# Chunk ends and first stage of a two-layer fp32 decoder rearranged: gate/up behind the down slabs, four plain pairs, squares on ScalarE

## Chip, cores and metric
One core of a Trainium2 chip runs the whole program. The metric is the device time in microseconds (us), here of single executions; the trace is one profiled execution of the kernel before.

## What is computed
Two macaron layers over 528 tokens (16 learned ones and 512 inputs) of width 1024, all in float32. FFN is a SwiGLU of inner width 2816, 22 slabs of 128.

```
def swiglu(x, w_gate, w_up, w_down):
    return (jax.nn.silu(x @ w_gate) * (x @ w_up)) @ w_down
...
h = concat(meta, x)
for l in range(2):
    h = h + 0.5 * swiglu(rmsnorm(h, ffn1_norm[l]), ...)
    h = h + mix(rmsnorm(h, mix_norm[l])) @ w_out[l]
    h = h + 0.5 * swiglu(rmsnorm(h, ffn2_norm[l]), ...)
y = rmsnorm(h, final_norm)[:, 16:]
```

(The loop is abridged; mix is a retention group beside a differential attention group. The change leaves it alone.)

## The kernel before
**Number format.** An fp32 product is made of three float32r matmuls: ScalarE copies the high half of an operand (`split`, L108, for weights; L327 for the inputs XH), VectorE subtracts for the low half (L109, and XL in L328), and TensorE adds hi x hi, lo x hi and hi x lo.

**Stages.** There are four FFN stages (two a layer), called stage 1 to 4 here, and a mix stage behind the first and the third. In each FFN stage, gate and up of one slab m of the inner width are a **pair**: two weight slabs of 512 KB, which `gu(m)` uses. The first PLAIN = 2 pairs of a stage are plain (`plain`, L518, 96 matmuls of 264 columns). All others go by one level of Strassen-Winograd: seven products P1 to P7 of four k steps and three matmuls each, 84 in all (`product`, L496), which `evacuate` adds up from PSUM: u1, u2 and u4 are copies on ScalarE (L455), L469 adds P2, L474 adds P5 into U, L476 and L477 make the gate from P3, L480 adds P4 and L481 multiplies; `split_hidden` makes the two halves hh (ScalarE, L551) and hl (VectorE, L552) of the result. Its weights need sums S1 to S4 of the quarters, which `sums` makes step by step: VectorE L129, L130 and L132, GpSimd L133.

**Chunks.** The 22 slabs are worked in three chunks, which end at 8, 16 and 22 (6, 14 and 22 in the last stage). After a chunk, `down` multiplies its hidden slabs by eight slabs of the down weights (L280), and evacuates each with L586 (times r/2) and L589 (added to h). `ffn_steps` sets the order: gate and up go one pair ahead, so that pair b of the next chunk runs before the down step of (a, b), and P5, P3 and P4 of that pair n come behind the down step, among the products of pair n + 1.

**Weights.** The class `Weights` goes down one list, `plan`, with three counters: transfers begun (`advance_dma`, four raw tiles of 512 KB, RAW_BUFS), splits made, slabs used. `step` is called between products and makes one step of the next slab's work; `take` hands a slab over. Tile pools set what waits for what, and a scheduler reorders the instructions of each engine within that.

**The start.** `start` loads the first slab in two halves between the inputs h[k]. Then, in a pool of their own, the inputs are scaled and split (`post_pair`), squared for the norm (`post_sq`: GpSimd squares six of eight slabs, L364, and adds with VectorE in turn, L369) and summed for Strassen (`post_sums`, L347 to L350), all before stage 1 begins. `norm_end` makes r = 1/rms (L413 last), which the first evacuation needs (L542).

```
for k in PAIRED:
    post_sq(k, FULL, k == 0, k == KD - 1, False, k % 4 < 3)
for k in range(4):
    post_sums(k, FULL, scratch)
```

## Time and profile before
| | |
|---|---|
| three runs | 2095.88, 2097.12, 2102.14 us; median 2097.12 |
| profiled execution | 2096.26 us, span 2094.5 us |
| mean granted TensorE clock | 0.992 of full speed |
| TensorE | 15238 matmuls, busy 2006.8 us |
| VectorE | 2292 instructions, busy 1573.0 us |
| ScalarE | 1506 instructions, busy 965.7 us |
| GpSimd | 286 instructions, busy 410.0 us |

The span runs from the first to the last instruction of the trace; the execution's own time is 1.8 us longer. A busy time is the sum of the engine's instructions; of TensorE, whose matmuls overlap and whose ends are modelled, the starts are the safer reading. Idle time counts only on the engine that the rest waits for.

### The profile page before, as it was taken

To read this page: it belongs to the slowest core of one execution; us is meant where nothing else is said; L and a number is where in the kernel's file an instruction comes from. 1 tells how busy PE (TensorE), PEld (TensorE's weight loads), DVE (VectorE), ACT (ScalarE), POOL (GpSimd) and SP (SyncE) were. 2 spreads that over 40 slices of the span, in tenths; PEclk is the share of its full clock that TensorE was granted. 3 is DMA by queue.
4 is the path that set the end of the run, shared out by engine and by line. 5 is a ranking of instruction groups with operands and counts; after the bars stand their busy time and mean duration, and the time that the engine had idled before them with its cause. 6 is when DMAs were issued, how large, how long until landed. Compare 5 with 4: busy or idle time off the path is not lost. (4 is left out here: it accounts for less than half of the span.)

```text
span 2094.5 us, 36936 instructions
## 1 busy us (share of the span) xinstructions
PE 2006.8 (96%) x15238; PEld 1930.9 (92%) x15238; DVE 1573.0 (75%) x2292; ACT 965.7 (46%) x1506; POOL 410.0 (20%) x286
## 2 busy tenths in 40 slices
PE   6999999999999999999989999999999999999996
PEld 5899999999999999999989999999888879898995
DVE  8867857668777886867698587766778789696765
ACT  5533525445446552543565254344554465353443
POOL 4100000344343100100110010004434331010002
PEclk8999999999999999999999999999999999999998
...
GB/s 153 91 131 52 121 81 95 120 68 64 57 61 90 89 123 70 95 129 68 94 102 102 91 91 116 67 99 114 66 62 62 70 81 101 101 101 121 80 104 49
DMA packets 57656, 190.08 MB, mean 91 GB/s; under 512 B 7056, under 2 KB 9104, under 8 KB 57488
## 3 DMA queue, kind: packets, MB, share of 16 engines
...
q8 instruction: 119, 1.95, 0.4%
q10 hardware_dynamic: 1024, 1.08, 0.3%
...
## 5 line engine op out<-in xcount | busy, mean ns | idle before, releaser
L133 POOL TENSOR_TENSOR ws<-ws,wraw 128x512 f32<-128x512 f32 x80 | 118.7, 1484 | 1101.0 <-DVE ws L132 931.8
L108 ACT ACTIVATE whi<-wraw 128x1024 fp32r<-128x1024 f32 (+1 forms) x180 | 184.8, 1032 | 274.7 <-PE pm L280 149.2
L496 PE MATMUL pm<-XH,xhi 128*128 128x264 f32 (+1 forms) x848 | 243.2, 287 | 11.0 <-DVE gu L474 5.4
L496 PE MATMUL pm<-XH,xlo 128*128 128x264 f32 (+1 forms) x848 | 240.5, 284 | 0.0
L496 PE MATMUL pm<-XL,xhi 128*128 128x264 f32 (+1 forms) x848 | 240.4, 283 | 0.0
L496 PE MATMUL pm<-XH,whi 128*128 128x264 f32 (+1 forms) x752 | 215.6, 287 | 6.8 <-DVE gu L474 6.6
L496 PE MATMUL pm<-XH,wlo 128*128 128x264 f32 (+1 forms) x752 | 213.1, 283 | 0.0
L496 PE MATMUL pm<-XL,whi 128*128 128x264 f32 (+1 forms) x752 | 213.0, 283 | 0.0
L109 DVE TENSOR_TENSOR wlo<-wraw,whi 128x1024 fp32r<-128x1024 f32 (+1 forms) x148 | 186.2, 1258 | 25.1 <-ACT whi L108 24.4
L280 PE MATMUL pm<-XH,whi 128*128 128x264 f32 (+1 forms) x768 | 181.1, 304 | 9.1 <-DVE ra L668 8.2
L280 PE MATMUL pm<-XL,whi 128*128 128x264 f32 (+1 forms) x768 | 178.7, 301 | 0.0
L280 PE MATMUL pm<-XH,wlo 128*128 128x264 f32 (+1 forms) x768 | 178.7, 302 | 0.0
L496 PEld LDWEIGHTS pm<-XH,xhi 128*128 128x128 f32 x848 | 159.5, 188 | 16.3 <-DVE gu L474 7.9
L496 PEld LDWEIGHTS pm<-XH,xlo 128*128 128x128 f32 x848 | 159.8, 188 | 0.3
L496 PEld LDWEIGHTS pm<-XL,xhi 128*128 128x128 f32 x848 | 159.9, 189 | 0.0
L496 PEld LDWEIGHTS pm<-XH,whi 128*128 128x128 f32 x752 | 141.4, 188 | 9.8 <-DVE gu L474 8.9
L496 PEld LDWEIGHTS pm<-XH,wlo 128*128 128x128 f32 x752 | 141.7, 188 | 0.2
L496 PEld LDWEIGHTS pm<-XL,whi 128*128 128x128 f32 x752 | 141.7, 188 | 0.0
L280 PEld LDWEIGHTS pm<-XH,whi 128*128 128x128 f32 x768 | 123.8, 189 | 16.9 <-issue 4.1
L108 ACT ACTIVATE xhi<-ws 128x1024 fp32r<-128x1024 f32 x84 | 88.9, 1058 | 103.7 <-PE pm L496 37.1
L108 ACT ACTIVATE whi<-ws 128x1024 fp32r<-128x1024 f32 x76 | 80.5, 1059 | 108.9 <-PE pm L496 45.2
L280 PEld LDWEIGHTS pm<-XL,whi 128*128 128x128 f32 x768 | 123.4, 189 | 4.7
...
## 6 DMA issues: line engine op xcount, KB each, us to landing
...
```

Of the source, the lines that this page charges most:

```text
L108: self.nc.scalar.activation(out=hi, in_=t, func=AF.Copy)
L109: (eng or self.nc.vector).tensor_tensor(out=lo, in0=t, in1=hi.bitcast(F32), op=ALU.subtract)
L133: nc.gpsimd.tensor_tensor(out=s4, in0=s2, in1=a12, op=ALU.add)
L280: nc.tensor.matmul(out=ps[:, o:o + c1 - c0], lhsT=a, rhs=b[:, c0:c1], start=start and n == 0, stop=stop and n == 2,)
L496: nc.tensor.matmul(out=out_, lhsT=p[:, s], rhs=q, start=k == 0 and n == 0 and what in ("P1", "P2", "P7"), stop=k == 3 and n == 2, skip_gro ...
```

## The change
- **Order of use.** `ffn_steps` now gives gate and up of a chunk, then its down step. The first pair of the next chunk runs behind the down slabs, but it is put into the list of transfers after DOWN_LEAD = 3 of the eight down slabs, and its sums are made during the down step. A second list, `use`, holds the order of use, and `step`, `ready` and `take` go by it.
- **Chunk ends.** P5, P3 and P4 of the chunk's last pair come among the first two slabs of the down step (`part`, `done`): half of slab 0 behind P5, the rest but the last k behind P3, slab 1 but its last k behind P4, then the last k of both.
- **Plain pairs.** Gate and up take turns at each of the eight input slabs (before: all of gate, then all of up). In stage 1 four pairs are plain (PLAIN_FIRST), two more than before: 24 matmuls more in all.
- **Start.** The first weight slab is one transfer ahead of the inputs, the second comes after two of them. Inputs are prepared in the pool of stage 1. The squares are on ScalarE, the adds all on VectorE, and `post_sums` comes behind the first plain pair.
- **Splits** of down slabs take their tiles from one pool in turn with the others (`parts_tile(False)`).

The diff, cut to its core:

```diff
@@ -41,15 +41,16 @@
 PLAIN = 2
+PLAIN_FIRST = 4
+DOWN_LEAD = 3
...
-    a = done = 0
+    a = 0
     for b in FFN_CHUNKS[kind]:
-        while done < min(b + 1, KF):
-            yield "gu", done
-            done += 1
+        for m in range(a, b):
+            yield "gu", m
         yield "down", (a, b), b == KF
@@ -64,8 +65,12 @@
-    def __init__(self, nc, pool, plan, ahead, dma_ahead):
-        self.nc, self.pool, self.plan = nc, pool, plan
+    def __init__(self, nc, pool, plan, use, ahead, dma_ahead):
+        self.nc, self.pool, self.plan, self.use = nc, pool, plan, use
+        self.turn_of = {i: u for u, i in enumerate(use)}
         self.ahead, self.dma_ahead = ahead, dma_ahead
@@ -74,16 +79,6 @@
-    def start(self):
-        srcs, n, kind = self.plan[0]
-        self.raw[0] = [self.raw_tile() for _ in srcs]
-        self.n_dma = 1
-        for t, src in zip(self.raw[0], srcs):
-            for c in (slice(0, 512), slice(512, 1024)):
-                self.nc.sync.dma_start(out=t[:, c], in_=src[:, c])
-                yield
@@ -161,7 +156,7 @@
                 )
-            parts = self.parts_tile(kind == "ffn")
+            parts = self.parts_tile(False)
             self.split([p[:, :n] for p in parts], t[:, :n], nc.gpsimd if kind == "mix" and i % 2 else None)
@@ -173,30 +168,34 @@
         i = self.n_split
-        if self.hold or i >= len(self.plan) or i > self.n_used + self.ahead:
+        if self.hold or i >= len(self.plan):
             return False
-        if self.plan[i][2] != "pair":
+        pair = self.plan[i][2] == "pair"
+        first = pair and self.plan[self.use[self.turn_of[i] - 1]][2] != "pair"
+        if self.turn_of[i] > self.n_used + (9 if first else 1 if pair else self.ahead):
+            return False
+        if not pair:
             self.advance_split(i + 1)
-        elif i <= self.n_used + (1 if self.plan[i - 1][2] == "pair" else 3):
+        else:
+            if first:
+                self.turn = 3
             self.n_split += 1
...
             next(self.gen)
-        else:
-            return False
         return True
     def ready(self, i):
-        while self.n_split <= i or self.gen is not None and self.at == i:
+        while i not in self.parts or self.gen is not None and self.at == i:
             assert self.step(), (i, self.n_split, self.n_used)
     def take(self):
-        i = self.n_used
-        if self.plan[i][2] == "pair":
-            self.ready(i)
-        else:
-            self.advance_split(i + 1 + self.ahead)
+        i = self.use[self.n_used]
+        upto = max(self.use[self.n_used:self.n_used + 1 + self.ahead]) + 1
+        if self.plan[i][2] != "pair":
+            self.advance_split(upto)
+        self.ready(i)
         self.n_used += 1
-        self.advance_dma(i + 1 + self.ahead + self.dma_ahead)
+        self.advance_dma(upto + self.dma_ahead)
         return self.parts.pop(i)
@@ -212,7 +211,10 @@
-    plan = []
+    def n_plain(l, f):
+        return PLAIN if l or f else PLAIN_FIRST
+    plan, use = [], []
     for l in range(DEPTH):
@@ -223,15 +225,20 @@
                     m, = args
-                    if m < PLAIN:
+                    if m < n_plain(l, f):
                         plan += [((wgu[l, f, m, i],), 1024, "plain") for i in range(2)]
+                    elif m not in FFN_CHUNKS[stage_kind(l, f)]:
+                        plan.append(((wgu[l, f, m, 0], wgu[l, f, m, 1]), 1024, "pair"))
                     else:
-                        plan.append(((wgu[l, f, m, 0], wgu[l, f, m, 1]), 1024, "pair"))
+                        at = len(plan) - KD + DOWN_LEAD
+                        plan.insert(at, ((wgu[l, f, m, 0], wgu[l, f, m, 1]), 1024, "pair"))
+                        use += [*range(len(use), at), *range(at + 1, len(plan)), at]
                 else:
...
                         plan.append(((wd[l, f, m, :, a * 128:b * 128],), (b - a) * 128, "ffn"))
-    W = Weights(nc, const, plan, 2, 2)
+    use += range(len(use), len(plan))
+    W = Weights(nc, const, plan, use, 2, 2)
@@ -353,19 +360,17 @@
-    def post_sq(m, mode, first, end, last=False, pool_squares=False):
+    def post_sq(m, mode, first, end, last=False, on_vector=False):
...
             nc.vector.tensor_tensor(out=sq, in0=hm, in1=hm, op=ALU.mult)
-        elif pool_squares:
-            nc.gpsimd.tensor_tensor(out=sq, in0=hm, in1=hm, op=ALU.mult)
         else:
...
         if not first and not apart:
-            add = nc.vector if end or pool_squares and m % 2 else nc.gpsimd
+            add = nc.vector if end or on_vector else nc.gpsimd
             add.tensor_tensor(out=total, in0=total, in1=sq, op=ALU.add)
@@ -431,7 +436,7 @@
-    def ffn(l, f, mode, g_next, kind):
+    def ffn(l, f, mode, g_next, kind, first=None):
         with tc.tile_pool(name=f"ffn{l}{f}", bufs=1, reuse_waits="tile") as pool:
@@ -449,6 +454,9 @@
+            if first is not None:
+                first(scratch)
@@ -503,6 +511,8 @@
+            np = n_plain(l, f)
@@ -521,14 +531,17 @@
-                if m < PLAIN - 1:
-                    for x in range(2):
-                        for i in range(0, KD, 2):
-                            half(x, 0, PAIRED[i:i + 2])
-                            half(x, 1, PAIRED[i:i + 2])
-                        if m == 0 and x == 0:
-                            norm_end(mode)
-                            act_table(SILU)
+                if m < np - 1:
+                    for k in PAIRED:
+                        for x in range(2):
+                            half(x, 0, (k,))
+                            half(x, 1, (k,))
+                    if m == 0:
+                        norm_end(mode)
+                        act_table(SILU)
+                        if first is not None:
+                            for k in range(4):
+                                post_sums(k, mode, scratch)
                 else:
@@ -560,39 +573,62 @@
             def gu(m):
-                if m < PLAIN:
+                if m < np:
                     plain(m)
-                    if m == PLAIN - 1:
+                    if m == np - 1:
                         for k in range(4):
                             post_t4(k, mode)
-                elif m == PLAIN:
-                    begin(m)
+                    return
+                begin(m)
+                n = m - 1
+                if n in state:
+                    rounds((("P5", n), ("P1", m), ("P2", m), ("P3", n), ("P6", m), ("P4", n), ("P7", m)))
+                else:
                     rounds((("P1", m), ("P2", m), ("P6", m), ("P7", m)))
-                else:
-                    begin(m)
-                    n = m - 1
-                    rounds((("P5", n), ("P1", m), ("P2", m), ("P3", n), ("P6", m), ("P4", n), ("P7", m)))
...
                 c0, c1 = ab
-                if final:
-                    n = KF - 1
-                    rounds((("P5", n), ("P3", n), ("P4", n)))
-                    act_table(LNEXP)
-                srcs = [hidden.pop(m) for m in range(c0, c1)]
+                n, nk = c1 - 1, c1 - c0
+                order = down_order(kind, final)
+                srcs = [hidden.pop(m) for m in range(c0, n)]
+                banks = {}
                 W.hold = final
-                for i, (m, md) in enumerate(down_order(kind, final)):
-                    P = project(md, srcs, ("pm", "pa")[i % 2])
+                def part(j, k0, k1):
+                    md = order[j][1]
+                    if j not in banks:
+                        banks[j] = pair(("pm", "pa")[j % 2]), W.take()
+                    ps, chunk = banks[j]
+                    for k in range(k0, k1):
+                        accumulate(ps, md, srcs[k:k + 1], chunk, k, nk)
+                        if k % 2:
+                            W.step()
+                def done(j):
+                    m, md = order[j]
+                    P = view(banks.pop(j)[0], md)
                     nc.vector.scalar_tensor_tensor(
...
                     nc.vector.tensor_tensor(out=cols(h[m], md), in0=cols(h[m], md), in1=P, op=ALU.add)
-                    if not final:
-                        W.step()
-                        continue
-                    post_h(m, g_next, md, kind, scratch)
-                    if g_next == 3 * DEPTH and m == KD - 1:
-                        finish(md)
+                    if final:
+                        post_h(m, g_next, md, kind, scratch)
+                        if g_next == 3 * DEPTH and m == KD - 1:
+                            finish(md)
+                product("P5", n)
+                part(0, 0, nk // 2)
+                product("P3", n)
+                part(0, nk // 2, nk - 1)
+                product("P4", n)
+                if final:
+                    act_table(LNEXP)
+                srcs.append(hidden.pop(n))
+                part(1, 0, nk - 1)
+                for j in range(len(order)):
+                    part(j, nk - 1 if j < 2 else 0, nk)
+                    done(j)
@@ -1005,12 +1041,12 @@
-    first = W.start()
-    next(first)
     nc.sync.dma_start(out=gain, in_=gains)
-    for k in PAIRED:
+    W.advance_dma(1)
+    for i, k in enumerate(PAIRED):
         nc.sync.dma_start(out=h[k], in_=hT[k])
-        next(first, None)
+        if i == 1:
+            W.advance_dma(2)
     W.advance_dma(4)
@@ -1021,18 +1057,17 @@
     act_table(LNEXP)
-    with tc.tile_pool(name="first", bufs=1, reuse_waits="tile") as pool:
-        scratch = lambda m: free_scratch(pool, m)
+    def first_inputs(scratch):
         W.advance_split(2)
...
         for k in PAIRED:
-            post_sq(k, FULL, k == 0, k == KD - 1, False, k % 4 < 3)
-        for k in range(4):
-            post_sums(k, FULL, scratch)
+            post_sq(k, FULL, k == 0, k == KD - 1, on_vector=True)
...
         last = l == DEPTH - 1
-        ffn(l, 0, FULL, 3 * l + 1, "mix")
+        ffn(l, 0, FULL, 3 * l + 1, "mix", None if l else first_inputs)
         if l == 0:
```

How the instructions move, at the three places that the prediction speaks of (of the kernel before and of the changed one, whose line numbers differ: L335 is the old L328, L354 to L357 the old L347 to L350, L374 the old L369, L104 the old L109, L504 the old L496, L565 the old L552, L611 and L614 the old L586 and L589).

First, VectorE's first instructions, before:

```order
L347 TENSOR_TENSOR xt<-xb_107 128x264
L109 TENSOR_TENSOR wlo<-wraw,whi 128x1024
L328 TENSOR_TENSOR XL<-xb_107,XH 128x528
L348 TENSOR_TENSOR xt<-xb_111,xb_107 128x264
L349 SCALAR_TENSOR_TENSOR xt<-xt,xb_111 128x264
L347 TENSOR_TENSOR xt<-xb_115 128x264
L348 TENSOR_TENSOR xt<-xb_119,xb_115 128x264
L350 SCALAR_TENSOR_TENSOR acc1h<-xt,xb_111 128x264
L328 TENSOR_TENSOR XL<-xb_111,XH 128x528
```

and now:

```order
L104 TENSOR_TENSOR wlo<-wraw,whi 128x1024
L354 TENSOR_TENSOR xt<-hh_106 128x264
L355 TENSOR_TENSOR xt<-ws_110,hh_106 128x264
L356 SCALAR_TENSOR_TENSOR xt<-xt,ws_110 128x264
L374 TENSOR_TENSOR acc<-acc,sq 128x528
L357 SCALAR_TENSOR_TENSOR acc1h<-xt,ws_110 128x264
L335 TENSOR_TENSOR XL<-hh_106,XH 128x528
L335 TENSOR_TENSOR XL<-ws_110,XH 128x528
L104 TENSOR_TENSOR wlo<-wraw,whi 128x1024
```

The first lo half of weights stands ahead of the sums (xt), and the adds of squares (acc) are among the first instructions, each on VectorE, where GpSimd squared and added beside it.

Second, TensorE in stage 1's third chunk, at the end of P1 of one pair (before pm_3569, now pm_3542) and the beginning of P3 of the pair ahead of it. Before:

```order
L496 MATMUL pm_3569<-XH_62,xlo_3396 128x264
L496 MATMUL pm_3569<-XL_63,xhi_3395 128x264
L496 MATMUL pa_3706<-XH_62,whi_3494 128x264
L496 MATMUL pa_3706<-XH_62,wlo_3495 128x264
L496 MATMUL pa_3706<-XL_63,whi_3494 128x264
L496 MATMUL pa_3706<-XH_62,whi_3494 128x264
L496 MATMUL pa_3706<-XH_62,wlo_3495 128x264
L496 MATMUL pa_3706<-XL_63,whi_3494 128x264
L496 MATMUL pm_3433<-XH_62,xhi_3389 128x264
```

and now:

```order
L504 MATMUL pm_3542<-XH_62,whi_3335 128x264
L504 MATMUL pm_3542<-XH_62,wlo_3336 128x264
L504 MATMUL pm_3542<-XL_63,whi_3335 128x264
L504 MATMUL pm_3410<-XH_62,xhi_3329 128x264
L504 MATMUL pm_3410<-XH_62,xlo_3330 128x264
```

Six matmuls of the next pair's P2 (pa) stood between the two, behind five others of it ahead of P1; now P3 follows P1 directly, and P2 stands elsewhere.

Third, VectorE at the final down step of stage 1. Slab 0's and 1's evacuations are those of the first pm and pa. Before:

```order
L552 TENSOR_TENSOR hl5_3970<-gu_3850,hh5_3969 128x528
L586 SCALAR_TENSOR_TENSOR pm_3974<-pm_3974,r_71 128x528
L586 SCALAR_TENSOR_TENSOR pa_4018<-pa_4018,r_71 128x528
L589 TENSOR_TENSOR slabs_61<-slabs_61,pm_3974 128x528
L109 TENSOR_TENSOR wlo_4170<-wraw_4073,whi_4169 128x768
L586 SCALAR_TENSOR_TENSOR pm_4068<-pm_4068,r_71 128x528
L589 TENSOR_TENSOR slabs_61<-slabs_61,pa_4018 128x528
L109 TENSOR_TENSOR wlo_4220<-wraw_4123,whi_4219 128x768
```

and now:

```order
L565 TENSOR_TENSOR hl5_3972<-gu_3819,hh5_3971 128x528
L611 SCALAR_TENSOR_TENSOR pm_3909<-pm_3909,r_71 128x528
L611 SCALAR_TENSOR_TENSOR pa_3976<-pa_3976,r_71 128x528
L614 TENSOR_TENSOR slabs_61<-slabs_61,pm_3909 128x528
L104 TENSOR_TENSOR wlo_3978<-wraw_3786,whi_3977 128x768
L611 SCALAR_TENSOR_TENSOR pm_4037<-pm_4037,r_71 128x528
L614 TENSOR_TENSOR slabs_61<-slabs_61,pa_3976 128x528
L104 TENSOR_TENSOR wlo_4039<-wraw_3910,whi_4038 128x768
```

Slabs counted from 0, the lo half behind the first add was that of slab 6 (wlo_4170); now it is that of slab 3 (wlo_3978), whose first matmuls stand 12 matmuls behind the last of slab 0 on TensorE.

## Rows read from the trace of the kernel before

**Rows 1.** The page: busy us (share of the span) x instructions.

```profile
PE 2006.8 (96%) x15238; PEld 1930.9 (92%) x15238; DVE 1573.0 (75%) x2292; ACT 965.7 (46%) x1506; POOL 410.0 (20%) x286
```

**Rows 2.** Stretches: length, busy us by engine, granted clock, DMA share, GB/s.

```profile
core 0: us, PE busy (x) PEld busy (x) DVE busy (x) ACT busy (x) POOL busy (x), PEclk, DMA share, GB/s
7.72:54.58 46.86, 32.17 (x197) 30.06 (x197) 45.34 (x60) 26.23 (x38) 23.24 (x11) 0.85 0.41 146
20.50:36.30 15.80, 8.38 (x35) 7.72 (x35) 15.80 (x20) 3.55 (x5) 8.16 (x5) 0.57 0.21 66
54.58:120.84 66.26, 62.77 (x505) 61.72 (x505) 55.79 (x81) 35.49 (x55) 7.17 (x6) 1.00 0.29 93
120.84:174.90 54.06, 54.06 (x446) 54.06 (x445) 30.24 (x40) 13.14 (x16) 2.57 (x2) 1.00 0.29 92
174.90:254.80 79.90, 76.84 (x613) 75.18 (x612) 68.76 (x96) 42.67 (x64) 8.17 (x6) 1.00 0.29 96
307.00:353.00 46.00, 45.84 (x374) 45.41 (x373) 38.95 (x57) 24.79 (x38) 3.87 (x3) 1.00 0.26 85
712.00:777.00 65.00, 62.42 (x506) 61.58 (x505) 55.02 (x81) 34.27 (x53) 6.53 (x5) 1.00 0.30 94
```

**Rows 3.** TensorE, 0 to 55 us: start, length, instruction [idle before, releaser].

```profile
7.72 0.59 PE L518 MATMUL pm<-XH,whi 128*128 128x264 f32 x1 [7.72 <-ACT XH L327]
...
15.13 0.59 PE L518 MATMUL pm<-XL,whi 128*128 128x264 f32 x1 [4.16 <-DVE XL L328]
...
26.32 0.59 PE L518 MATMUL pm<-XL,whi 128*128 128x264 f32 x1 [5.77 <-DVE XL L328]
...
54.58 0.36 PE L496 MATMUL pm<-XH,xhi 128*128 128x264 f32 x1 [2.02 <-DVE gu L542]
```

**Rows 4.** VectorE, 5 to 33 us, the same columns.

```profile
11.02 1.53 DVE L349 SCALAR_TENSOR_TENSOR xt<-xt,xb 128x264 f32<-128x264 f32 x1
...
14.99 0.42 DVE L349 SCALAR_TENSOR_TENSOR xt<-xt,xb 128x264 f32<-128x264 f32 x1
...
15.96 0.70 DVE L369 TENSOR_TENSOR acc<-acc,sq 128x528 f32<-128x528 f32 x1
...
17.54 0.97 DVE L328 TENSOR_TENSOR XL<-xt,XH 128x792 fp32r<-128x792 f32 x1
...
27.65 1.82 DVE L328 TENSOR_TENSOR XL<-xb,XH 128x528 fp32r<-128x528 f32 x1
...
30.07 1.21 DVE L109 TENSOR_TENSOR wlo<-wraw,whi 128x1024 fp32r<-128x1024 f32 x1
31.21 0.69 DVE L328 TENSOR_TENSOR XL<-xb,XH 128x528 fp32r<-128x528 f32 x1
```

**Rows 5.** GpSimd, 16 to 23 us, the same columns.

```profile
16.73 5.52 POOL L364 TENSOR_TENSOR sq<-slabs 128x528 f32<-128x528 f32 x1 [3.26 <-DVE acc L369]
```

**Rows 6.** DMA in 0 to 30 us, 40 equal slices.

```profile
GB/s 0 0 131 265 203 266 301 309 296 372 335 403 408 424 422 432 410 426 377 379 246 22 0 0 0 0 0 0 0 0 0 0 0 0 93 333 273 0 0 0
```

**Rows 7.** TensorE at a stop in stage 1 and one in stage 2.

```profile
191.88 0.39 PE L496 MATMUL pm<-XH,xhi 128*128 128x264 f32 x1 [1.69 <-DVE gu L474]
...
735.41 0.39 PE L496 MATMUL pm<-XH,whi 128*128 128x264 f32 x1 [1.30 <-DVE gu L474]
```

**Rows 8.** TensorE's waits, 712 to 777 us: in total, times, longest.

```profile
PE pm L496 <- DVE gu L474: 2.6, 4, 1.3
```

**Rows 9.** VectorE at a wait in stage 1's second chunk.

```profile
189.57 0.69 DVE L130 TENSOR_TENSOR ws<-wraw 128x512 f32<-128x512 f32 x1 [3.41 <-DMA wraw<-in_wgu]
```

**Rows 10.** VectorE at the final down step of stage 1.

```profile
379.32 0.72 DVE L586 SCALAR_TENSOR_TENSOR pm<-pm,r 128x528 f32<-128x528 f32 x1 [2.90 <-PE pm L280]
379.95 0.71 DVE L586 SCALAR_TENSOR_TENSOR pa<-pa,r 128x528 f32<-128x528 f32 x1
380.56 0.69 DVE L589 TENSOR_TENSOR slabs<-slabs,pm 128x528 f32<-128x528 f32 x1
381.17 0.95 DVE L109 TENSOR_TENSOR wlo<-wraw,whi 128x768 fp32r<-128x768 f32 x1
```

## The prediction

> **What bounds the kernel now.** I read the page's busy line first: TensorE is busy 96% of the span [rows 1], so time is lost only where TensorE stands or runs at its lower clock. Next, the table by stage [rows 2], for where TensorE stands. The stretch 120.84 to 174.90 has no idle time at all: 446 matmuls in 54.06 us, a pace of 0.1212 us for 264 columns. I take that pace for full speed and call **excess** what a stretch lasts beyond matmuls times pace. It is 46.86 - 197 x 0.1212 = 23.0 us in stage 1's plain pairs, and by the same sum 5.0 us in the pairs behind them, 5.6 in its second chunk, 0.7 in its third, and 3.7 in the first chunk of stage 2. The down stretch itself has none.
>
> The start's rows say why. TensorE begins at 7.72 us, stops for 4.16 us before 15.13 and for 5.77 us before 26.32, both times for a lo half from VectorE (XL, L328), and once more for 2.02 us before the first Strassen product at 54.58, on the gate's evacuation L542 [rows 3]. In 20.5 to 36.3 VectorE is busy all the 15.80 us and the granted clock is 0.57, which is a mix of 1.2 GHz, the lower of two levels, and 2.4 GHz [rows 2]. VectorE is slow there because GpSimd squares beside it: one and the same sum (L349) takes 1.53 us at 11.02 and 0.42 at 14.99 [rows 4], while one square stretches to 5.52 us [rows 5].
>
> **The start.** First matmul: the other 256 KB of the first weight slab now land ahead of h[0]; at the 203 to 266 GB/s of these first microseconds [rows 6] that is 1.0 to 1.3 us, so the first matmul moves from 7.72 to about 9.
>
> VectorE's list, from the order: up to the eighth XL of the inputs it holds three 128x1024 lo halves, 14 sums of 264 columns, 8 XL of 528, two of 792, five adds of 528 and little else. Undisturbed rows give 1.21, 0.42, 0.69, 0.97 and 0.70 us [rows 4], less the 0.08 by which neighbours overlap (1.14 from 30.07 to 31.21): 3.4 + 4.8 + 5.0 + 1.8 + 3.1 = 18.1 us, from 6.5 to about 25, where the old kernel has its last such XL at 31.21. Taking the squares off GpSimd is what does it: nine VectorE instructions beside it, to the XL of 1.82 us at 27.65, lasted some 0.8 to 1.1 us longer than alone, as the two L349 show: about 8.6 in all. Against that, all seven adds now stand on VectorE, where three did: 4 x 0.62 = 2.5 us more. Squares go to ScalarE, busy 26.23 of 46.86 us [rows 2]; eight more fit beside VectorE's list and cost nothing, unless an add waits for its square.
>
> One section speaks against this. The Trainium skill, "Perfetto Trace Analysis", section "Optimizing Scalar/DVE Operations", says that a saturated VectorE may be relieved by giving work to ScalarE or even GpSimd, with the reservation that GpSimd shares VectorE's port. By its first half the change would only lose the 2.5 us; by its reservation, and the rows, it gains.
>
> TensorE then takes gate and up in turn per slab, so each XL feeds 12 matmuls instead of 6, and it no longer comes to an XL before it is made: by 28 us the first 100 matmuls are through, at full clock by about 22. Behind them 288 plain matmuls wait for nothing but r, whose chain now starts with the adds at once. I allow 1.0 us for that wait, and the 2.02 us wait at 54.58 goes, as two more plain pairs cover r's chain. 28 + 288 x 0.1212 + 1.0 = 64 us. The Strassen pairs 4 to 7 follow, 336 x 0.1212 = 40.7 us, with about 2 us of stalls: 107. The old kernel has 700 of its matmuls behind it at 120.84, and these are 724, so the 24 extra matmuls of two plain pairs (2.9 us) are inside. **Start: -14 us** (-8, if the low clock stays to 36 us as before; -16, if no stall is left).
>
> **The pair loop.** In the old third chunk, between the previous pair's P4 and this pair's P3 on TensorE stand 47 matmuls, because part of the next pair's P2 fell in there; now it is 36, and 24 for a chunk's second pair (the order ahead shows the piece). Meanwhile VectorE must evacuate P4 (L480), multiply (L481), make two lo halves and hl and only then do L474, which P3 waits for. That is the order of the old first chunk of stage 2, and its row has the price: a stop of 1.30 us, 1.47 with the matmul's own handover, at the second pair [rows 7], and with the later ones 2.6 us of idle in 4 waits [rows 8]. That is 0.43 each for these three, and with the same handover of 0.17 I take 0.6. The last two pairs of a chunk have none.
> - First chunks of stages 2 to 4: 1.47 + 2 x 0.6 and 0.4 of small gaps = 3.1 against 3.7: -0.6 x 3 = -1.8.
> - Second chunks: 1.47 + 5 x 0.6 + 0.4 = 4.9 against 5.6, where VectorE's wait of 3.41 us for a raw tile [rows 9] goes, since the next pair's tiles are now fetched in the down stage: -0.7 x 4 = -2.8.
> - Third chunks of stages 1 to 3: 1.47 + 2 x 0.6 + 0.4 = 3.1 against 0.7: +2.4 x 3 = **+7.2**. The last stage's third chunk had that already.
>
> **The chunk ends.** P5, P3 and P4 of a chunk's last pair now stand among the first slabs. Behind P4 come ScalarE's hh and VectorE's hl, covered by some 31 matmuls of the next slabs (3.8 us): nothing, since in the old final down VectorE stood 2.90 us behind the same hl, before slab 0 was done [rows 10]. Then slabs 0 and 1 end together, and VectorE's list is L611, L611, L614 and only then the lo half of slab 3's weights. The same four stand in the old final down at 379.32 to 382.12 [rows 10], 2.8 us, and with the handover I count 3.05. At stage 1's final down 12 matmuls between slab 0's last and the first with that lo half cover it (1.46 us): about 1.65 us of stall, in three stages **+5.0** (the last stage stops at this place already). At the eight other ends some 24 matmuls cover it (2.9 against 3.3 with the wider lo half): 0.5 each, **+4.0**.
>
> The next pair's sums, moved into the down stage, issue two 512 KB transfers, three VectorE sums and a GpSimd sum each. VectorE is busy 30.24 of 54.06 us in such a stretch [rows 2], so I cost them at nothing; without that cover it would be the lo halves of the later slabs that come late. Mix stages keep their order on every engine: nothing.
>
> **The sum.** -14 - 1.8 - 2.8 + 7.2 + 5.0 + 4.0 = -2.4 us. The profiled execution took 2096.26 (0.9 below the median of the runs), so **2094 us**. A measurement of this kernel tells 0.3%, 6.3 us, from no change: forecast no difference, though for a reason: a large gain at the start, given back in eleven chunk ends and three third chunks.
>
> **Rivals.**
> - *The new waits don't come* (chance 0.30). For it: the stalls of the loop and of the ends are margins of 0.4 to 1.6 us between two chains, and my chain lengths are sums of steps. Without the chunk ends it is 2096.3 - 14 + 2.6 = 2085; without the third chunks' +7.2 too, 2078.
> - *The start gains half* (0.13). A slower ramp, low clock to 36 us: 2096.3 - 8 + 11.6 = 2100. Against it: nothing on VectorE's list is left that a GpSimd operation delays.
> - *Raw tiles* (0.15; slower). There are four. From slab 3 on the next pair holds two of them until its splits, so that each down slab has one of two. A transfer is 2 us at the 266 GB/s of [rows 6], the two halves of a split about 1.1 each; a slab of eight lasts 48 matmuls, 5.8 us. It decides when a split falls behind two evacuations and an add (1.8 us more): then the chain passes 5.8, and each late tile costs what the 3.41 us wait cost in the second chunk, where TensorE stopped for 1.69 us at 191.88 on the L474 behind it [rows 7]. Once per non-final down, eight times: +13.5, 2094 + 13.5 = 2107.5. Against it: the DMA share is 0.29 there [rows 2], and the tiles were ordered long before they are split.
>
> **Numbers.** Forecast (2088 to 2101) 0.42, the rivals 0.30, 0.13 and 0.15. Below 2090 lie the first rival and a little of the forecast's lower edge on a better start: 0.38. Above 2102.6 the last: 0.15. Within: 0.47. The range reaches from 2079 to 2105; below it is some 0.05 of the first rival, above most of the last.
>
> **What would show it.** Right: no GpSimd squares, VectorE's 264-column sums at 0.42 us from the first on, a granted clock near 1 from some 22 us on, the first Strassen product near 64 us and the end of pair 7 near 107; stops of 1.3 us on L482 (the old L474) at the second pair of every chunk, third chunks with some 3 us of excess; at final downs a stop of 1.5 us on the lo half of slab 3. Wrong: a first product behind 70 us, third chunks without stops, or waits for raw tiles in the down stretches.

## The result, and the profile after

The changed kernel takes 2127.69 us (median of 4 runs, 2124.47 to 2129.12) against 2099.63 of the kernel before in the same comparison (4 runs, 2095.88 to 2112.32). The ratio is 1.0121, its 95% interval 1.0075 to 1.0166: slower, by some 28 us, and outside the range of the forecast. The profiled execution took 2129.12 us.

The page's first line, which answers to [rows 1], shows 13 us more of busy TensorE, of which the 24 matmuls are 2.9:

```profile
PE 2020.0 (95%) x15262; PEld 1937.3 (91%) x15262; DVE 1556.1 (73%) x2278; ACT 962.9 (45%) x1502; POOL 394.5 (19%) x274
```

Where the time went is read from stretches that begin with TensorE's first matmul of a stage (columns as in [rows 2]). The kernel before, stage 1, mix, stages 2 and 3, mix, last stage with the tail:

```profile
0.00:398.99 398.99, 369.87 (x2932) 364.51 (x2933) 297.50 (x410) 179.26 (x260) 60.83 (x44) 0.98 0.31 101
398.99:688.08 289.09, 283.55 (x2263) 278.32 (x2261) 215.53 (x359) 143.72 (x264) 114.12 (x80) 0.99 0.24 78
688.08:1054.74 366.66, 361.15 (x2934) 358.18 (x2933) 274.56 (x388) 167.23 (x244) 34.05 (x24) 1.00 0.29 93
1054.74:1428.39 373.65, 362.40 (x2934) 358.47 (x2933) 283.18 (x395) 168.57 (x245) 42.33 (x29) 1.00 0.30 96
1428.39:1716.73 288.34, 276.58 (x1726) 245.11 (x1725) 219.31 (x333) 138.19 (x242) 111.68 (x80) 0.99 0.23 75
1716.73:2094.50 377.77, 353.24 (x2459) 326.33 (x2457) 282.95 (x411) 168.69 (x253) 46.99 (x32) 0.98 0.29 94
```

The changed kernel, the same stretches:

```profile
0.00:392.35 392.35, 368.75 (x2955) 363.52 (x2956) 282.65 (x395) 176.75 (x256) 37.55 (x32) 1.00 0.32 103
392.35:682.99 290.64, 285.10 (x2262) 279.88 (x2261) 215.79 (x359) 143.96 (x265) 114.64 (x80) 0.99 0.24 77
682.99:1057.83 374.84, 362.89 (x2934) 358.44 (x2933) 275.45 (x390) 167.46 (x244) 39.81 (x25) 1.00 0.29 92
1057.83:1438.48 380.65, 364.96 (x2934) 360.01 (x2933) 281.57 (x392) 167.45 (x245) 41.45 (x29) 1.00 0.29 94
1438.48:1729.24 290.76, 277.85 (x1727) 246.07 (x1726) 220.30 (x333) 138.27 (x243) 111.01 (x80) 0.99 0.23 74
1729.24:2127.40 398.16, 360.43 (x2460) 329.38 (x2458) 280.31 (x411) 169.02 (x253) 50.06 (x32) 0.97 0.28 89
```

Stage 1 is 6.6 us shorter, though it has 24 matmuls more. Stage 2 is 8.2 longer, stage 3 7.0, the last stage 20.4. The two mix stages, whose instructions stand in the same order, are 1.6 and 2.4 longer; between the kernels below they vary from 288 to 293 us with no change to them, so nothing is read from that.

**The start came as forecast.** Stretches and stops of the changed kernel, which answer to [rows 2] and [rows 3]:

```profile
10.27:64.02 53.75, 50.61 (x388) 49.42 (x388) 49.25 (x74) 35.95 (x53) 4.29 (x2) 1.00 0.47 158
20.50:36.30 15.80, 14.91 (x121) 14.64 (x121) 15.00 (x22) 11.24 (x16) 0.00 (x0) 1.00 0.30 95
64.02:107.00 42.98, 41.68 (x338) 41.08 (x337) 30.90 (x46) 20.33 (x32) 3.62 (x3) 1.00 0.20 62
```

```profile
10.39 0.59 PE L528 MATMUL pm<-XH,whi 128*128 128x264 f32 x1 [10.39 <-ACT XH L334]
...
11.72 0.59 PE L528 MATMUL pm<-XL,whi 128*128 128x264 f32 x1 [0.52 <-DVE XL L335]
...
18.28 0.39 PE L528 MATMUL pm<-XL,whi 128*128 128x264 f32 x1 [0.79 <-DVE XL L335]
...
34.24 0.36 PE L528 MATMUL pa<-XH,whi 128*128 128x264 f32 x1 [0.89 <-DVE sq L413]
```

The first matmul starts at 10.4 (forecast: 9), the stops for XL are 0.52 and 0.79 us where they were 4.16 and 5.77, and the granted clock in 20.5 to 36.3 is 1.00 where it was 0.57. The first Strassen product starts at 64.02 and 388 + 338 matmuls are through at 107, as forecast; the kernel before had 700 at 120.84. That is the -14 us.

**The pair loop** has the stops that were forecast, in the second and third chunks of each stage and in the first of stages 2 and 3. One of stage 1's third chunk, and all those on L482 (the old L474; the kernel before has 12.0 us in 16 there):

```profile
313.65 0.39 PE L504 MATMUL pm<-XH,whi 128*128 128x264 f32 x1 [1.29 <-DVE gu L482]
```

```profile
PE pm L504 <- DVE gu L482: 21.6, 28, 1.5
```

**The chunk ends** lost far more than forecast. Stage 1's final down step: TensorE's stops, then VectorE and ScalarE behind them ([rows 10] shows VectorE there before):

```profile
362.96 0.48 PE L287 MATMUL pm<-hh,whi 128*128 128x264 f32 x2 [0.62 <-DVE gu L488]
...
370.18 0.48 PE L287 MATMUL pm<-hh,whi 128*128 128x264 f32 x2 [0.62 <-DVE slabs L614]
370.96 0.51 PE L287 MATMUL pa<-hh,wlo 128*128 128x264 f32 x2 [0.29 <-DVE wlo L104]
```

```profile
362.38 0.43 DVE L488 TENSOR_TENSOR gu<-pm,rc 128x264 f32<-128x264 f32 x1 [0.73 <-PE pm L504]
...
368.10 0.72 DVE L611 SCALAR_TENSOR_TENSOR pm<-pm,r 128x528 f32<-128x528 f32 x1 [3.05 <-PE pm L287]
368.73 0.71 DVE L611 SCALAR_TENSOR_TENSOR pa<-pa,r 128x528 f32<-128x528 f32 x1
369.34 0.70 DVE L614 TENSOR_TENSOR slabs<-slabs,pm 128x528 f32<-128x528 f32 x1
369.95 0.95 DVE L104 TENSOR_TENSOR wlo<-wraw,whi 128x768 fp32r<-128x768 f32 x1
```

```profile
368.15 2.31 ACT L103 ACTIVATE whi<-wraw 128x768 fp32r<-128x768 f32 x3 [3.84 <-PE pm L287]
```

Slab 2 begins 0.62 us late because its PSUM bank is the one that P4 has just filled, and L488 reads it at 362.38. Then ScalarE makes three high halves in one go at 368.15, having waited 3.84 us for TensorE to end slab 0. Slab 3's lo half (369.95) follows VectorE's two evacuations and an add without a pause, as the forecast had it, and TensorE waits 0.29 us for it; the 0.62 us before that, at 370.18, are slab 4's wait for the bank of slab 0. In the last stage the same place costs more; the end of its first chunk:

```profile
1807.17 0.47 PE L287 MATMUL pm<-hh,whi 128*128 128x512 f32 x1 [0.61 <-DVE gu L488]
...
1813.52 0.49 PE L287 MATMUL pa<-hh,whi 128*128 128x512 f32 x1 [0.52 <-ACT whi L103]
1815.20 0.47 PE L287 MATMUL pm<-hh,whi 128*128 128x512 f32 x1 [1.19 <-DVE slabs L614]
1815.98 0.50 PE L287 MATMUL pa<-hh,wlo 128*128 128x512 f32 x1 [0.31 <-DVE wlo L104]
```

```profile
1812.62 2.31 ACT L103 ACTIVATE whi<-wraw 128x768 fp32r<-128x768 f32 x3 [4.14 <-PE pm L287]
```

```profile
1813.78 0.69 DVE L611 SCALAR_TENSOR_TENSOR pm<-pm,r 128x512 f32<-128x512 f32 x1
...
1814.97 0.95 DVE L104 TENSOR_TENSOR wlo<-wraw,whi 128x768 fp32r<-128x768 f32 x1
```

Here slabs 0, 1 and 2 end together, so that VectorE has three evacuations (the third at 1813.78) and an add ahead of slab 3's lo half, where it has two and an add in stages 1 to 3. At the ends of the second and third chunk the granted clock falls as well, behind the last of these stops (columns as in [rows 2]):

```profile
1944.00:1947.40 3.40, 3.40 (x9) 2.67 (x10) 3.27 (x4) 0.00 (x0) 0.00 (x0) 0.51 0.64 171
2080.50:2083.90 3.40, 3.40 (x9) 2.63 (x8) 3.40 (x4) 2.69 (x5) 2.38 (x2) 0.50 0.71 178
```

The eight or nine matmuls of 512 columns in each stretch start some 0.43 us apart where 0.231 is the pace, 1.6 to 1.7 us lost each time.

From all starts of TensorE's matmuls I sum the **excess** as in the forecast (each start-to-start time less the pace: 0.121, 0.117 and 0.231 us for 264, 256 and 512 columns), over the stretches of Strassen products (loops) and over the rest of the FFN stages behind the plain pairs (ends; 7 us of the last stage's are the norm at the tail, in every kernel). Time at the lower granted clock is part of the excess. The medians come from several comparisons, in which the kernel before had 2097.30 to 2099.67 us, so that a difference of 2 or 3 us between two rows is not told from none. An excess is that of the profiled execution, which for lead_in_x (2101.42) lies 5.6 us below the median:

| kernel | median us | loops, 12 chunks | ends, stages 1, 2, 3, last | ends in all |
|---|---|---|---|---|
| before | 2099.63 | 46.9 | 1.1, 1.1, 1.1, 11.7 | 15.0 |
| changed | 2127.69 | 53.1 | 6.3, 6.2, 6.2, 27.5 | 46.2 |
| start_only | 2090.05 | 45.6 | 1.1, 1.1, 1.1, 11.7 | 15.0 |
| ends_only | 2136.36 | 54.2 | 6.2, 6.2, 6.2, 28.4 | 47.0 |
| pool_alone | 2121.44 | 64.5 | 4.9, 4.9, 4.9, 13.6 | 28.3 |
| final_two_pools | 2120.99 | 51.4 | 5.0, 4.8, 4.8, 24.3 | 38.9 |
| lead_in_x | 2107.01 | 48.1 | 2.2, 2.1, 2.2, 18.5 | 25.0 |
| banks_swapped | 2122.10 | 51.7 | 7.9, 6.2, 7.6, 24.7 | 46.4 |
| both_mends | 2114.02 | 52.2 | 3.7, 3.6, 3.8, 20.1 | 31.2 |
| p2_held | 2108.34 | 45.1 | 4.1, 4.3, 4.1, 22.7 | 35.2 |
| p2_held_start | 2097.96 | 52.1 | 1.5, 1.3, 1.3, 11.2 | 15.3 |
| pool_alone_held | 2093.47 | 47.2 | 1.0, 0.9, 0.9, 14.8 | 17.6 |

The changed kernel has 31.2 us more than the one before at the ends and 6.2 in the loops (9.2, if stage 1's first chunk, which is counted with the start, is left out).

### The profile page after: what moved, and what is told of

The parts are those of the page before. It is cut to its first block, busy times and chain, and to the rows that moved or that the text cites. A ratio compares the mean times of both kernels' runs of the same rounds, so it can differ in the third digit from the quotient of the medians.

```text
span 2127.4 us, 36899 instructions
## 1 busy us (share of the span) xinstructions
PE 2020.0 (95%) x15262; PEld 1937.3 (91%) x15262; DVE 1556.1 (73%) x2278; ACT 962.9 (45%) x1502; POOL 394.5 (19%) x274
## 5 line engine op out<-in xcount | busy, mean ns | idle before, releaser
L103 ACT ACTIVATE whi<-wraw 128x1024 fp32r<-128x1024 f32 (+1 forms) x229 | 232.6, 1026 | 359.2 <-PE pm L287 121.7
L104 DVE TENSOR_TENSOR wlo<-wraw,whi 128x1024 fp32r<-128x1024 f32 (+1 forms) x197 | 250.3, 1274 | 72.9 <-ACT whi L103 72.1
L504 PE MATMUL pm<-XH,xhi 128*128 128x264 f32 (+1 forms) x780 | 224.9, 288 | 21.2 <-DVE gu L482 7.1
L504 PE MATMUL pm<-XH,whi 128*128 128x264 f32 (+1 forms) x780 | 224.7, 288 | 15.3 <-DVE gu L482 14.4
L504 PE MATMUL pm<-XH,xlo 128*128 128x264 f32 (+1 forms) x780 | 222.0, 285 | 0.0
L504 PE MATMUL pm<-XL,xhi 128*128 128x264 f32 (+1 forms) x780 | 221.9, 285 | 0.0
L504 PE MATMUL pm<-XH,wlo 128*128 128x264 f32 (+1 forms) x780 | 221.7, 284 | 0.0
L504 PE MATMUL pm<-XL,whi 128*128 128x264 f32 (+1 forms) x780 | 221.5, 284 | 0.0
L504 PEld LDWEIGHTS pm<-XH,xhi 128*128 128x128 f32 x780 | 147.3, 189 | 27.5 <-DVE gu L482 10.0
L504 PEld LDWEIGHTS pm<-XH,whi 128*128 128x128 f32 x780 | 147.4, 189 | 20.2 <-DVE gu L482 17.4
L287 PE MATMUL pm<-hh,whi 128*128 128x264 f32 (+2 forms) x624 | 144.4, 300 | 12.4 <-DVE gu L488 7.4
L287 PE MATMUL pa<-hh,wlo 128*128 128x264 f32 (+2 forms) x624 | 147.6, 303 | 5.6 <-DVE wlo L104 5.5
L504 PEld LDWEIGHTS pm<-XH,wlo 128*128 128x128 f32 x780 | 147.7, 189 | 0.3
L504 PEld LDWEIGHTS pm<-XL,xhi 128*128 128x128 f32 x780 | 147.9, 190 | 0.0
L504 PEld LDWEIGHTS pm<-XH,xlo 128*128 128x128 f32 x780 | 147.8, 189 | 0.1
L504 PEld LDWEIGHTS pm<-XL,whi 128*128 128x128 f32 x780 | 147.7, 189 | 0.0
L287 PE MATMUL pa<-hh,whi 128*128 128x264 f32 (+2 forms) x624 | 144.9, 301 | 2.0 <-ACT whi L103 2.0
```

The source lines that it names most:

```text
L103: self.nc.scalar.activation(out=hi, in_=t, func=AF.Copy)
L104: (eng or self.nc.vector).tensor_tensor(out=lo, in0=t, in1=hi.bitcast(F32), op=ALU.subtract)
L287: nc.tensor.matmul(out=ps[:, o:o + c1 - c0], lhsT=a, rhs=b[:, c0:c1], start=start and n == 0, stop=stop and n == 2,)
L504: nc.tensor.matmul(out=out_, lhsT=p[:, s], rhs=q, start=k == 0 and n == 0 and what in ("P1", "P2", "P7"), stop=k == 3 and n == 2, skip_gro ...
```

## Experiments

The theory at this point: the start gives what was forecast, and the loss lies in the new order at the chunk ends. Rivals: that the plain pairs in turn lose it, that the PSUM banks do, and that the tiles for split weights do. On the last, the diff has one line, `parts_tile(False)`: down slabs are split into one pool of three pairs of tiles, where two pools of three took turns.

**start_only** undoes everything but the start, the plain pairs and gate and up in turn: `ffn_steps`, the plan, `take`, `gu` and `down` are the old ones, and the split tiles come from two pools.

```diff
     for b in FFN_CHUNKS[kind]:
-        for m in range(a, b):
-            yield "gu", m
+        while done < min(b + 1, KF):
+            yield "gu", done
+            done += 1
         yield "down", (a, b), b == KF
...
-            parts = self.parts_tile(False)
+            parts = self.parts_tile(kind == "ffn")
```

> The changed kernel with the old order of gate/up and down, the old down step and the old two pools for split weights; start, four plain pairs and gate/up in turn are kept. Theory (the start gains what was forecast, the chunk ends and pair loops lose more than twice what was forecast): the first Strassen product stays near 64 us, 724 matmuls are through near 107 where the kernel before had 700 at 120.84 (-14), and gate/up in turn costs some 2 us at the first Strassen pair of stages 2 to 4: about 2085 us, against 2097 of the kernel before. Rival (the changed start or the plain pairs in turn lose time in all stages): 2097 or more. The stops on the evacuation of P4 and on lo halves at chunk ends should be absent, and the third chunks should have 0.7 us of excess again.

Measured: 2090.05 us, ratio to before 0.9963 (0.9948 to 0.9977), first Strassen product at 63.5, loops and ends as before in the table. It beats both kernels, the one before by 7.3 us in their common comparison (2097.30). Of the expected 2085, 5 us are missing; in the profiled execution the second mix stage is 4 us longer than in the kernel before and the last stage 2.6.

**ends_only** is the counterpart: the kernel before with the new order of use, down step and pool.

> The kernel before with the new order of gate/up and down, the new down step and the single pool; the start, two plain pairs and gate before up are the old ones. Theory: all of the loss is here, about 2127 + 14 - 2 = 2139 us, with the same stops as in the changed kernel: 1.45 us at the second pair of second and third chunks, 0.78 at the third slab, lo halves late at the ends, and 5 to 7 us per chunk end in the last stage. Rival (part of the loss comes from plain pairs in turn or from the start): below 2125.

Measured: 2136.36, ratio 1.0185 (1.0165 to 1.0204). So both halves add up to within 4 us (39.1 lost here against its own comparison, 7.3 gained by start_only, 28.1 lost in the changed kernel), and the whole loss, some 39 us, is in order, down step and pool.

**banks_swapped:**

```diff
-                        banks[j] = pair(("pm", "pa")[j % 2]), W.take()
+                        banks[j] = pair(("pa", "pm")[j % 2]), W.take()
```

> The changed kernel, with the two PSUM tags of the down slabs swapped (pa for slab 0, pm for slab 1), so that slab 2 takes a bank that was evacuated long before and no longer the one that P4 has just filled. Theory that the 0.78 us stops before slab 2 are a wait for that bank alone: they go at all twelve ends, -9 us, about 2118. Rival (the wait is one of several that end at nearly the same time, and the split weights of slab 3 are late anyway): the stop moves to the next slab, -3 us or less, about 2125.

Measured: 2122.10, ratio 1.0116 (1.0099 to 1.0133). The stops before slab 2 are gone, but the ends keep 46.4 us: the stop moved to slab 3's weights, as the rival has it. Of the 5.6 us gained, 5 lie in the mix stages of the profiled run.

**final_two_pools** and **lead_in_x** give tiles back. The first splits the down slabs of a stage's last chunk into both pools in turn; the second puts the first three slabs of every chunk into the stage's own tiles.

```diff
-            parts = self.parts_tile(False)
+            parts = self.parts_tile(kind == "last ffn")              # final_two_pools
+            parts = self.parts_tile(False, kind == "ffn x")          # lead_in_x: slabs 0 to 2, tag x
...
```

> The changed kernel, with the down slabs of each stage's last chunk split into two pools in turn again, as before the change (six pairs of tiles where the changed kernel has three). Theory that a single pool with three tiles makes slab 3's split wait until slab 0 is done: the stops behind slabs 0 and 1 (0.79 and 0.46 us in stages 1 to 3, 0.89, 1.24 and 0.81 in the last) and the stop before slab 2 go, since slab 3 can be worked meanwhile: -2.0 x 3 and about -4 in the last stage, about 2118 us. Rival (VectorE's order behind the evacuations is the cause, not the tiles): no change, 2127.

> The changed kernel, with the first three down slabs of each chunk split into the stage's own three tiles and the other five into the common three, where the changed kernel has all eight in the common three. Theory (the loss at chunk ends is that slab 3 cannot be split while slabs 0 to 2 are held open): the stops behind slab 2 go in all stages, with the 5 to 7 us per chunk end of the last stage, -15 to -20 us, about 2110. Rival (the ends lose by the hidden half's chain from P4 on, whatever is split): 2122 or more.

Measured: 2120.99 (ratio 1.0116, 1.0095 to 1.0137) and 2107.01 (1.0036, 1.0023 to 1.0049): 6.7 and 20.7 us come back, with the ends from 46.2 to 38.9 and 25.0. ScalarE at the final down step of stage 1 in final_two_pools:

```profile
353.56 0.83 ACT L103 ACTIVATE whi<-wraw 128x768 fp32r<-128x768 f32 x1
...
360.08 0.85 ACT L103 ACTIVATE whi<-wraw 128x768 fp32r<-128x768 f32 x1 [5.04 <-PE pm L504]
...
370.01 1.58 ACT L103 ACTIVATE xhi<-wraw 128x768 fp32r<-128x768 f32 x2 [3.71 <-PE pm L287]
```

Five high halves of these slabs, from 340.90 to 360.08, are now made ahead of slab 0's end, where the changed kernel has three, from 346.20 to 359.82; only later slabs' stay behind. What lead_in_x keeps in the last stage is one long stop a chunk, of slab 4 for the PSUM bank of slab 0, whose evacuation comes late because slabs 0 to 3 end together (2.48 us in the first chunk, 1.64 in the others):

```profile
1800.61 0.50 PE L289 MATMUL pm<-hh,whi 128*128 128x512 f32 x1 [2.48 <-DVE slabs L616]
```

**pool_alone** puts the single pool into start_only, in the old order, and nothing else.

```diff
-            parts = self.parts_tile(kind == "ffn")
+            parts = self.parts_tile(False)
```

> The kernel with the new start and the old order of gate/up and down (2090.05 us), with the single pool of three tiles for split down slabs and nothing else of the new chunk ends. Theory A (three tiles cost time only together with the new ends, where slabs 0 and 1 are both kept open until the last pair's hidden half is ready): 2090, with at most 2 us at each final down step: up to 2096. Theory B (three tiles are by themselves the cause of most of the loss): above 2110.

Measured: 2121.44, ratio 1.0109 (1.0094 to 1.0124): theory B, which I had not held. 31 us by one line. TensorE's waits on the evacuation of P5, start_only and then pool_alone:

```profile
PE pm L492 <- DVE gu L470: 10.5, 14, 1.5
```

```profile
PE pm L492 <- DVE gu L470: 31.1, 45, 1.5
```

14 stops have become 45. The order of instructions says how: between P4 of one pair and P3 of the next, in the third chunk, TensorE has in start_only

```
P7 and P5: 24   P2: 5   P1: 12   P2: 6   = 47 matmuls
```

and in pool_alone

```
P7 and P5: 24   P1: 12   = 36 matmuls
```

(P7 and P5 are of P3's own pair, P1 of the pair behind it, P2 of the pair behind that.) P2's place is the difference: in start_only eleven matmuls of it cover VectorE behind P4, in pool_alone all of it stands ahead of P4, and P3 waits. Whether P2's place is the whole of the 31 us, pool_alone_held below tests.

The line does two things. Down slabs have three pairs of tiles where they had six. And `parts_tile(True)` changes the pool after every three splits, a count in which the eight down slabs took part: in the old kernel the three splits of one pair lie in both pools behind a stage's first down step, now every pair has one pool to itself. That is how a stage's first chunk stood all along, and there the old order had the 36 matmuls and the stops too (stage 2 of the kernel before [rows 8]: 2.6 us in 4). I take the second effect for the reason that P2's weights are split early and the scheduler puts P2 first. No run has the two effects apart. But final_two_pools and lead_in_x give tiles back and leave each pair its own pool, and both keep the stops:

```profile
PE pm L504 <- DVE gu L482: 23.9, 32, 1.5
```

```profile
PE pm L506 <- DVE gu L484: 27.0, 39, 1.5
```

**both_mends** (swapped banks and final_two_pools) and **lead_in_x_banks** (swapped banks and lead_in_x):

> The changed kernel with swapped banks and with two pools at the final down steps. If the two causes are separate the gains add: 2127.7 - 5.6 - 6.7 = 2115 us. If they are one cover that is short in two ways, the second adds little: 2120.

> The changed kernel with the first three down slabs of each chunk in the stage's own tiles (2107.01 us), with the two PSUM tags of the down slabs swapped as well. Theory (behind the tiles, the banks are what is short: slab 2 waits for P4's bank, 0.7 us, and slab 4 for that of slab 0, 1.8 to 2.6 us in the last stage): the first kind goes at all ends, the second stays, -6 us, 2101. Rival (the first kind moves into the second): 2106 or more.

Measured: 2114.02 (ratio 1.0075, 1.0059 to 1.0090) and 2103.65 (1.0023, 1.0013 to 1.0033). The first is near the sum of the two gains, by luck: at the ends the swap alone gave nothing (46.4 against 46.2), and where slab 3's tiles are there it gains 7.7 (31.2 against 38.9). With lead_in_x it gains 3.4 us, between the two expectations.

**p2_held** and **p2_held_start** keep P2 behind P1 by an ordering rule.

```diff
+                        if what == "P2" and k == n == 0:
+                            tc.add_manual_dep(mm.ins, st["P1"].ins.name, nosync, reason="P2 behind P1")
...
```

> The changed kernel with one ordering rule more: the first matmul of P2 stays behind P1 of its pair on TensorE, so that P2 can't move ahead of the previous pair's P4 and lies between P4 and P3 again. Theory (P3's cover, 36 matmuls instead of 47, is the cause of the loop's stops): the 28 waits on L482 (21.6 us idle, some 26 start to start) go nearly all, about 2105. Rival (VectorE's list as a whole is too long in these stretches): the waits move to other evacuations, -8 us or less, about 2120.

> The kernel with the new start and the old order of gate/up and down (2090.05 us) with the same ordering rule for P2. Its 14 waits on the evacuation of P5 are 10.5 us of idle: theory 2079, rival 2088 or more.

Measured: 2108.34 (ratio 1.0049, 1.0033 to 1.0066) and 2097.96 (0.9999, 0.9990 to 1.0008). In the changed kernel 19 us come back, 8 in the loops and 11 at the ends. In start_only the rule loses 8 us, a plain miss: the stops on L470 stay (10.5 us before, 11.4 now), and waits for ScalarE come to them. TensorE's waits of p2_held, then of p2_held_start:

```profile
PE pm L504 <- ACT rc L463: 27.0, 39, 0.8
```

```profile
PE pm L492 <- ACT rc L451: 15.4, 28, 0.8
PE pm L492 <- DVE gu L470: 11.4, 15, 1.3
```

Both now wait most for ScalarE's copy of u (rc). The rule moves more than P2. The products of p2_held in stage 1's third chunk, the slab in brackets:

```
P5(18) P1(19) P2(19) P6(19) P3(18) P7(19) P5(19) P4(18) P3(19) P1(20) P2(20) P4(19)
```

P3(19) follows P4(18) directly, where the kernel before has some 47 matmuls between such two, and P5(19) stands ahead of P4(18). So P2 has not come back to its old place, as the expectation had it: the scheduler has made a third order.

**lead_in_x_held** adds the rule to lead_in_x:

> The changed kernel with both: the first three down slabs in the stage's own tiles, and P2 behind P1. If the chunk ends and the loop are separate losses: 2127.7 - 17 - 22 = 2089 us, within 0.5% of the kernel with the new start and the old order (2090). If a third cause is left in the new order of use: above 2100.

Measured: 2102.54 (ratio 1.0022, 1.0012 to 1.0033). Alone the two gave 20.7 and 19.4 us back, together 25.2: to a large part they are one gain.

**pool_alone_held** is pool_alone with the rule: one pool, but P2 behind P1.

> pool_alone (start_only with the single pool of split tiles, 2121.4 us, 64.5 us of excess in the loops, 28.3 at the ends) with the ordering rule that keeps P2 behind P1. Theory: the pool costs its 18.9 us in the loops only through P2's move ahead of P4. Then the rule takes the pool's part away: the loops come to those of p2_held_start, 52 us, the waits on the evacuation of P5 (31.1 us in 45) to its 11.4 in 15, the ends keep some 28, and the kernel takes about 2121.4 - 12.5 = 2109. Rival: the pool also makes the sums' splits late by itself, whatever P2's place. Then the loops stay above 58 us and the time above 2115. If the ends fall too, below 22 us, then their loss in pool_alone came from P2's place as well, and the time is nearer 2100.

Measured: 2093.47, ratio 0.9974 (0.9965 to 0.9982). 28.0 of the 31.4 us come back, 17.3 of them in the loops and 10.7 at the ends: the last case that the expectation names, and 7 us beyond it. The waits on L470, 31.1 us in pool_alone, are no longer among the first of TensorE's list, which is now led by

```profile
PE pm L492 <- ACT rc L451: 19.7, 32, 0.8
```

So the single pool costs nothing by itself: with the rule, one pool takes 2093.47 and two take 2097.96 (p2_held_start). What costs is the order that the scheduler makes of it when P2 is free, and stages 1 to 3 lose by it at their ends too. That the eleven matmuls of P2 are the whole reason is not shown, as the rule sets the other products anew too (from P1(19) on, the piece of p2_held's order above stands here too); stage 1's third chunk keeps 3.4 us of excess, where pool_alone has 4.0 and start_only 1.6, and the gain is largest in the second chunks.

With this run a chain of steps leads from before to the changed kernel, in medians: the start, 2099.63 to 2090.05, -9.6; the pool with P2 held (pool_alone_held, two edits at once), +3.4; the order of use and the new down step (p2_held), +14.9; P2 let go (the changed kernel), +19.4. By each run's ratio to the kernel before in its own comparison the steps are -7.8, +2.3, +15.7 and +15.1. The sizes hang on the path: from pool_alone, where P2 is free, the order of use and the new down step add 6.3 us (2121.44 to 2127.69), 17.9 more at the ends and 11.4 less in the loops.

**ylo_gpsimd** moves one lo half from VectorE to GpSimd.

```diff
-        self.split([p[:, 0:512] for p in g4], a22)
+        self.split([p[:, 0:512] for p in g4], a22, nc.gpsimd)
```

> The changed kernel with the lo half of A22 (128x512, 0.6 us on VectorE) made on GpSimd, so that VectorE's list between the evacuation of P4 and that of the next P5 is one step shorter. Theory that this list sets the 28 stops on L482: each is 0.6 us shorter, the small ones go, -10 to -17 us, about 2114. Rival (GpSimd takes longer, disturbs VectorE's additions beside it and makes P4 late): 2127 or more.

Measured: 2140.26, ratio 1.0196 (1.0179 to 1.0214). The rival: the lo half takes 1.69 us on GpSimd (median) where VectorE took 0.68, the loops hold 62.6 us of excess where the changed kernel has 53.1, and the waits on L482, 21.6 us there, rose.

```profile
PE pm L504 <- DVE gu L482: 25.1, 28, 2.0
```

**start_gate_first** goes back to gate before up in the first plain pair of stages 2 to 4; **start_squares_gpsimd** and **start_plain_two** take the start apart. All three are made from start_only.

```diff
+        elif on_vector and m % 4 < 3:                                  # start_squares_gpsimd
+            nc.gpsimd.tensor_tensor(out=sq, in0=hm, in1=hm, op=ALU.mult)
-            add = nc.vector if end or on_vector else nc.gpsimd
+            add = nc.vector if end or on_vector and m % 2 else nc.gpsimd
-PLAIN_FIRST = 4
+PLAIN_FIRST = 2                                                        # start_plain_two
```

> The kernel with the new start and the old order of gate/up and down (2090.05 us), with all of gate before up in the first plain pair of stages 2 to 4, as in the kernel before. Theory that gate and up in turn make the gate's evacuation late, for which the first Strassen pair waits (1.0 us in stage 2 and 2.4 in the last stage, and 0.5 more inside it): 2086 us, and these stops go. Rival (the waits come from r or from split weights): 2090.

> The kernel with the new start and the old order of gate/up and down (2090.05 us), with six of the eight squares and half of their adds on GpSimd again, as in the kernel before. Theory (GpSimd beside VectorE is what made the old start slow): the stops before XL come back, the first Strassen product moves from 63.5 to about 70 us, 2097. Rival (gate and up in turn and the later sums give the gain, whoever squares): 2090, first Strassen product below 66.

> The same kernel with two plain pairs in stage 1 instead of four: 24 matmuls fewer, 2.9 us. Theory that the two more plain pairs pay only by covering the chain of r: r is ready near 37 us and two plain pairs end near 40, so that little waits: 2088 us. Rival (XL of the sums T1 to T3 and the first Strassen sums are not ready by then): a wait of 3 us or more before the first Strassen product, 2092 or more.

Measured: start_gate_first 2093.33 (ratio 0.9978, 0.9968 to 0.9988), no gain; the wait before the first Strassen pair does not come from the order of gate and up. r is now made behind the whole first plain pair and may be what is late, but this was not tried. start_squares_gpsimd: 2096.48 (0.9985, 0.9975 to 0.9995), the theory: the first Strassen product moves to 68.3 us and the old stops are back (the longest of 3.67 us), with VectorE at 1.29 us for a sum of 264 columns:

```profile
13.02 0.59 PE L518 MATMUL pm<-XL,whi 128*128 128x264 f32 x1 [3.67 <-DVE XL L323]
```

```profile
10.18 1.29 DVE L344 SCALAR_TENSOR_TENSOR xt<-xt,ws 128x264 f32<-128x264 f32 x1
```

start_plain_two: 2094.67 (0.9979, 0.9969 to 0.9989). Neither theory, though the time is the rival's: TensorE waits 3.5 us for the norm within the plain pairs (2.35 and 1.19), and not before the first Strassen product. The medians put four pairs ahead by 4.6 us, the ratios by 3.4, the profiled stage 1 by 1.5.

## Why the prediction failed, by its own steps

- **The start: right.** -14 us was forecast; at the end of pair 7 it was 13.8 in the trace, with first product and end of pair 7 at the times given. In the median of start_only 7.3 are left against its own comparison (9.6 against 2099.63), as its second mix stage and last stage are longer. The reason holds too: with the squares back on GpSimd 6.4 us are lost again (4.6 by the ratios). The Trainium skill, "Perfetto Trace Analysis", section "Optimizing Scalar/DVE Operations", makes the reservation that GpSimd and VectorE share a port, so that moving work between them might not help. The trace agrees: a sum lasts 1.29 us beside GpSimd in start_squares_gpsimd and 0.42 alone [rows 4].
- **The pair loop: price right, cause wrong.** Third chunks were put at +2.4 each and measured +2.6 (3.6 against 1.0 in stage 1), with the stop of 1.29 us at the second pair. The last stage's third chunk, put at nothing, has 1.8 more (6.4 against 4.6). The first chunks of stages 2 to 4 and the second chunks were to gain 4.6; together they gained 0.4. VectorE's waits for raw tiles did fall, but TensorE gained nothing by it. And the order of use is not needed for the stops: pool_alone has them in the old order, by the one line on the pool. VectorE's waits for raw tiles, before and then changed (us in all, times, longest):

```profile
DVE ws L130 <- DMA wraw<-in_wgu: 32.3, 29, 3.4
...
DVE ws L129 <- DMA wraw<-in_wgu: 10.9, 7, 1.8
```

```profile
DVE ws L124 <- DMA wraw<-in_wgu: 9.4, 9, 1.5
...
DVE ws L125 <- DMA wraw<-in_wgu: 3.6, 10, 0.5
```

- **The chunk ends: the step that failed.** "The same four stand in the old final down ... in three stages +5.0 (the last stage stops at this place already). At the eight other ends ... 0.5 each, +4.0": 9 us were forecast and 31.2 measured: 15.4 in stages 1 to 3, where 8 stood, and 15.8 in the last stage, where 1 stood (its final end at nothing because it stopped there before, its two others at 0.5). I priced VectorE's list behind slabs 0 and 1, which came as forecast, and not what stands beside it. Split tiles: three hold slabs 0, 1 and 2, all open until the last pair's hidden half is there, so ScalarE can't split slab 3 before slab 0 ends (3.84 us of waiting at 368.15). PSUM: slab 2 has P4's bank, 0.6 us at each of twelve ends, and slab 4 that of slab 0. In the last stage a third slab ends with the two, and at two of its ends the clock falls. Some 11 us of the 31.2 go when P2 is held (p2_held, 35.2 against 46.2 at the ends). Against pool_alone_held, with the same pool and the same rule, 17.6 are left that belong to the order of use and the down step, where I had 9; against pool_alone 17.9.
- **One line of the diff had no term in the sum: the other step that failed.** `parts_tile(False)` stood in the list of edits, and I gave it neither a price nor a cover. It costs 31 us in the old order, 18.9 in the loops and 13.3 at the ends, through the order that it lets the scheduler make. In the changed order holding P2 gives 19 back; the changed order with the old turn of the pools throughout was not run. I had read from the order that P2 moved, and laid its price (2.4 us) on three third chunks alone.
- **The rivals.** *Raw tiles* had the right sign and the wrong resource: the tiles that were short at the ends were those of split weights, behind the raw ones. *The new waits don't come* fell with the trace, and *the start gains half* too: the low clock to 36 us that it rests on did not come, though the 7.3 us of start_only's median are near its 8.
- The Trainium skill, "Perfetto Trace Analysis", section "Optimization Strategy", says that the same gap repeated on the engine that should be saturated can mean that there isn't room in SBUF or PSUM for the next tile. The trace agrees: 0.62 us before slab 2 at each end is a bank, and three splits at once behind slab 0 are split tiles.

Open: how much of the last stage's 15.8 us the third slab explains (the clock is some 3.3 of them), which of the pool's two effects moves P2, and what makes r or the gate's evacuation late in stages 2 and 4.
